# Eight activation buffer pairs of a two-layer decoder trunk, each 32 bytes longer

## The chip, the cores and the metric

The kernel runs on one core of a Trainium2 chip. The metric is the time of one execution on the device in microseconds (us), as the median of several runs. The engines are TensorE (PE, with its weight loads listed apart as PEld), VectorE (DVE), ScalarE (ACT), GpSimd (POOL) and SyncE (SP), which issues the DMAs here.

## What is computed

Two layers of a decoder trunk on 256 positions of 1024 channels, in float32. Each layer is a SwiGLU feed-forward network (FFN), a mixer, and a second FFN. The mixer of layer 0 pools over windows of 2, 4, 8 and 16 positions. The mixer of layer 1 is attention over one block of 256 positions, on keys and values that are made from the stream between the layers. The part that matters here, four times over, is

```python
def swiglu(h, w_in, w_out):
    gu = h @ w_in
    g, u = jnp.split(gu, 2, axis=-1)
    return (jax.nn.silu(g) * u) @ w_out
# D_MODEL 1024, D_FF 2816, SEQ 256; in each layer:
h = modulate(rms_norm(x, norm_g[layer, 0]), sh, sc)
x = x + MACARON_WEIGHT * (1.0 + g)[:, None, :] * swiglu(h, ffn_w_in[layer, 0], ffn_w_out[layer, 0])
```

## The kernel before

**Tiling.** Channels lie on the 128 partitions and the 256 positions along the free dimension. The 2816 inner channels of an FFN are 22 tiles of 128, numbered j. For each j the first half of an FFN (`gstep`, L464) makes one PSUM tile `gu` of 2 × 256 columns out of 8 tiles of the input `h`. `evac` (L414) makes `silu(g) * u` of it. The second half (`ystep`, L481) multiplies that by 8 weight slices of 128 × 128 (numbered m) into the four PSUM tiles `y`, which hold all 1024 output channels and are summed over the 22 j.

**Three matmuls for one.** Each float32 operand is cut into a part `hi` of type float32r and a rest `lo`. `mm3` (L255) then makes a product out of three matmuls of 256 columns: L256 streams the activation's hi over the weights' hi, L259 the activation's lo over the weights' hi, and L260 the activation's hi over the weights' lo. Each of the three loads its 128 × 128 weights (the stationary operand) and streams its activations (the moving operand) past them. The profile names them so that `y<-acth,hi` streams `acth` over the weights `hi`.

**Activation buffers.** `new_act` (L410) takes a pair `acth`, `actl` of 128 × 256 float32r from the pool `ax`, which has eight buffers of each, used in turn. ACT writes `acth` (L129, or L438 for the first three j of FFNs 1 to 3) and DVE writes `actl` (L130, L441). The pooling mixer takes its tiles `z` from the same buffers (`scaled`, L805), and `v_job` (L942) keeps the attention's values in them. There they are the stationary operand: of the matmuls `py<-at,z` (L816) and of `att<-ph,acth` (`weighted`, L989).

**Weights.** The `Stream` objects load raw weights by DMA into `raw` and cut them (L168 on ACT, L169 on DVE) into `hi` and `lo`, with two buffers of each for the first half of an FFN (8192 bytes) and two for the second (4096 bytes).

**Order.** The order on PE and SP is that of the code, and FFN starts and mixers follow the tables `PROGRAM`, `MIXER` and `ATTENTION`. In between a `g` step of 48 matmuls and a `y` step of 24 alternate; jobs such as `evac` run a step later.

**Addresses.** Within a partition the built program puts the buffers at these bytes. The eight `acth` stand 1024 bytes apart from 16576 on, and the eight `actl` from 24768 on. All sixteen leave 192 when divided by 256. All `hi` and `lo` buffers leave 160, and the weight slices in them begin at multiples of 512 bytes. The two `h` tiles `hhi` and `hlo` leave 192, with 1024 bytes from one of the 8 parts to the next, and so do the hkv tiles. The tiles `room0`, `room1` and `room2`, which nothing writes or reads, shift the buffers behind them by 64, 64 and 128 bytes.

Of the kernel before, what the change touches and what calls it, by code (L numbers as in the profile page):

```python
# [7 lines left out]
F32 = mybir.dt.float32  # L8
F32R = mybir.dt.float32r
# [4 lines left out]
P = 128  # L14
D = 1024
KT = D // P
T = 256
# [69 lines left out]
def trunk(ctx: ExitStack, tc: tile.TileContext, xin, cin, small, ada, kvada, win0a, win1a, win0b,  # L87
# [3 lines left out]
    ax = ctx.enter_context(tc.tile_pool(name="ax", bufs=8))  # L91
# [13 lines left out]
    def nm(s):  # L105
        uid[0] += 1
        return f"{s}_{uid[0]}"
# [17 lines left out]
    def psum(tag, name):  # L125
        return pp.tile([P, 512], F32, tag=tag, name=nm(name), bufs={"y": 4, "g": 3, "m": 1}[tag])
# [182 lines left out]
    def a_of(s, m):  # L309
        return acol[:, s * KT + m:s * KT + m + 1]  # L310
# [8 lines left out]
    def square2(src):  # L319

        sq = new_2t("sq")
        nc.scalar.activation(sq, src, AF.Square)
        return sq
# [9 lines left out]
    def sums(o, tiles):  # L333
        for i, sq in enumerate(tiles):
            for t in range(TT):
                nc.tensor.matmul(o[:, t:t + 1], sq[:, t * P:(t + 1) * P], ones[:, 0:1],
                                 start=(i == 0 and t == 0), stop=(i == len(tiles) - 1),
                                 skip_group_check=True)

    def rinv(acc, n, mul, add, tag="r", bufs=2):  # L340
        ms = tp.tile([P, 4], F32, tag="ms", name=nm("ms"))[:, :n]
        r = tp.tile([P, 4], F32, tag=tag, name=nm("r"), bufs=bufs)[:, :n]
        nc.vector.tensor_scalar(ms, acc, mul, add, op0=ALU.mult, op1=ALU.add)
        nc.gpsimd.tensor_tensor(r, ms, nhalf[:, :n], op=ALU.pow)  # L344
        return r
# [41 lines left out]
    def new_xa(s, n=KT):  # L387
        xh = cp.tile([P, KT, T + 2], F32R, tag="kxhi", name=nm("xah"))
        xl = cp.tile([P, KT, T + 2], F32R, tag="kxlo", name=nm("xal"))
        xa_shift((xh, xl), s, 0, n)  # L390
        return xh, xl
# [6 lines left out]
    def xa_parts(xa, m, s):  # L398
        hi = xa[0][:, m, 0:T]
        return (lambda: nc.scalar.activation(hi, xT[:, m, :], AF.Copy, scale=a_of(s, m)),  # L400
                lambda: nc.vector.scalar_tensor_tensor(
                    out=xa[1][:, m, 0:T], in0=xT[:, m, :], scalar=a_of(s, m), in1=hi.bitcast(F32),
                    op0=ALU.mult, op1=ALU.subtract))
# [4 lines left out]


    def new_act():  # L410
        return (ax.tile([P, T], F32R, tag="acth", name=nm("acth"), bufs=8),
                ax.tile([P, T], F32R, tag="actl", name=nm("actl"), bufs=8))

    def evac(act, j, ps):  # L414
        sl = tp.tile([P, T], F32, tag="sl", name=nm("sl"), bufs=3)
        act[j] = new_act()
        nc.scalar.activation(sl, ps[:, 0:T], AF.Silu)  # L417
        nc.vector.tensor_mul(sl, ps[:, T:2 * T], sl)  # L418
        hilo(sl, *act[j])
        yield  # L420
# [95 lines left out]
    def add_x(m, yv, s):  # L516
        nc.vector.scalar_tensor_tensor(out=xT[:, m, :], in0=yv, scalar=gcol[:, s * KT + m:s * KT + m + 1],
                                       in1=xT[:, m, :], op0=ALU.mult, op1=ALU.add)
# [17 lines left out]
    def fold_steps(sq):  # L536

        def fold(other):
            nc.vector.tensor_add(sq[0][:, 0, :], sq[0][:, 0, :], other())

        def pair(k, e):
            e.tensor_tensor(sq[0], sq[0], sq[k], op=ALU.add)

        return {"P1": lambda: pair(1, nc.gpsimd), "P2": lambda: pair(2, nc.gpsimd),
                "D2": lambda: pair(2, nc.vector), "D3": lambda: pair(3, nc.vector),
                "F0": lambda: fold(lambda: sq[0][:, 1, :])}

    def yview(y, m):
        return y[m // 2][:, (m % 2) * T:(m % 2 + 1) * T]

    def run(program, steps):

        split = {}
        for name in program.split():
            if name[0] == "w":
                k, piece = name[1:3], int(name[4])
                if k not in split:
                    split[k] = sa.cuts() if k[0] == "a" else [] if sb.ready else sb.cuts()
                if piece < len(split[k]):
                    split[k][piece]["hl".index(name[3])]()  # L560
            elif name in steps:
                steps[name]()
# [89 lines left out]
    with tc.tile_pool(name="xp", bufs=XBUFS) as xpool:  # L652
# [110 lines left out]
        act = {}  # L763
# [19 lines left out]
        def mixer():  # L783
            last()
            xs = cp.tile([P, KT, T], F32, tag="kxhi", name="xs")
            ss = psum("m", "ss")[:, T:T + TT]
            pw = sa.raw.pop(0)[0]
            sq, got, zps, zs, yp = {}, {}, {}, {}, {}
            steps = {}

            def group_map(g, ts=range(TT)):
                if 0 in ts:
                    zps[g] = psum("g" if g < 3 else "y", "z")
                for t in ts:
                    for i in range(2):
                        kt = 2 * g + i
                        nc.tensor.matmul(zps[g][:, t * T:(t + 1) * T], xs[:, kt, t * P:(t + 1) * P],  # L797
                                         pw[:, kt * T:(kt + 1) * T], start=(t == 0 and i == 0),
                                         stop=(i == 1), skip_group_check=True)
                if g == NG - 1:  # L800
                    sa.load()

            def scaled(g, t):

                zs[g, t] = ax.tile([P, T], F32, tag="act" + "hl"[t], name=nm("z"), bufs=8)  # L805
                nc.scalar.activation(zs[g, t], zps[g][:, t * T:(t + 1) * T], AF.Copy,
                                     scale=got["r"][:, t:t + 1])

            def pooled(g):

                yp[g] = psum("y", "py")
                for i in range(2):
                    o, c = yp[g][:, i * T:(i + 1) * T], slice(i * P, (i + 1) * P)
                    for t, to, a in ((0, slice(0, P + BAND), at[:, g, 0:P + BAND]),
                                     (1, slice(P, T), at[:, g, P + BAND:AW])):
                        nc.tensor.matmul(o[:, to], zs[g, t][:, c], a, start=(i == t == 0),  # L816
                                         stop=(t == 1), skip_group_check=True)

            def square(k):
                sq[k] = square2(xT[:, 2 * k:2 * k + 2, :])  # L820

            def begin():
                sq.clear()
                got["xa"] = new_xa(2)
                for m in range(KT):
                    steps[f"H{m}"], steps[f"L{m}"] = xa_parts(got["xa"], m, 2)

            def fold(a, b):
                nc.vector.tensor_add(a, a, b)

            steps.update(fold_steps(sq))
            steps.update({"E": lambda: fold(sq[3][:, 0, :], sq[3][:, 1, :]),
                          "F1": lambda: fold(sq[0][:, 0, :], sq[3][:, 0, :]),
                          "G2": lambda: group_map(2, [0]), "k2": lambda: group_map(2, [1])})
            for m in range(KT):
                steps[f"A{m}"] = lambda m=m: add_x(m, yview(y, m), 0)
                steps[f"X{m}"] = lambda m=m: nc.scalar.activation(xs[:, m, :], xT[:, m, :], AF.Copy,
                                                                  scale=a_of(1, m))
                steps[f"B{m}"] = lambda m=m: add_x(m, yp[m // 2][:, m % 2 * T:(m % 2 + 1) * T], 1)
            for g in range(NG):  # L840
                steps[f"Q{g}"] = lambda g=g: square(g)
                steps[f"g{g}"] = lambda g=g: group_map(g)
                steps[f"y{g}"] = lambda g=g: pooled(g)
                for t in range(TT):
                    steps[f"z{g}{t}"] = lambda g=g, t=t: scaled(g, t)
            steps.update({"S": lambda: sums(ss, [sq[0][:, 0, :]]),
                          "R": lambda: got.update(r=rinv(ss, TT, 1.0 / D, EPS)), "N": begin})
            run(MIXER, steps)
            return {k: steps[k] for k in ("L6", "L7")}, got["xa"], lambda: [sq[0][:, 0, :]]
# [90 lines left out]
    def v_job(c, pv):  # L940
        for t in range(TT):
            vt[c, t] = new_act()  # L942
            hilo(pv[:, t * T:(t + 1) * T], *vt[c, t])
        yield
# [207 lines left out]
```

## Time and profile before

| | us |
|---|---|
| median of 3 runs | 897.16 |
| the three runs | 894.82, 897.16, 897.55 |
| the profiled execution | 894.96 |
| its span, first to last instruction | 892.8 |
| PE busy / DVE busy / ACT busy in it | 879.4 / 717.1 / 453.0 |

All that is said of the trace comes from the profiled execution. Its time is 2.2 us over its span, and 2.2 us under the median of the runs. In the page, a matmul's listed duration (around 0.28 us) is longer than the distance to the next one's start, since matmuls are pipelined. So what one matmul costs is read from the starts: two starts in the timeline, and the number of matmuls between them.

### The profile page before, as it was taken

How to read it: one execution, taken by the hardware profiler on the slowest of the kernel's cores; microseconds unless marked ns; L12 is line 12 of the kernel's file. 1: busy time of each engine (PE TensorE's matmuls, PEld its weight loads, DVE VectorE, ACT ScalarE, POOL GpSimd, SP SyncE). 2: the span in 40 equal slices, each digit the busy share in tenths (PEclk: the TensorE clock that was granted, in tenths of full speed). 3: DMA queues.
4: the chain of work that ended last, by engine and by line, in shares of the span. 5: the costliest groups of instructions: out<-in, count | busy, mean ns of one | idle time of the engine just before them, and what ended most of it. 6: DMA issues, size and time to landing. Idle time of an engine off the chain costs nothing.

```text
span 892.8 us, 17826 instructions
## 1 busy us (share of the span) xinstructions
PE 879.4 (99%) x7398; PEld 873.0 (98%) x7398; DVE 717.1 (80%) x1212; ACT 453.0 (51%) x721; POOL 49.4 (6%) x52
## 2 busy tenths in 40 slices
PE   6999999999999999999999999999999999999998
PEld 4999999999999999999999999999999999999998
DVE  5988988878998878869998888789888894665553
ACT  3456344328744444457554443457676674443431
POOL 0000000002000000000000000034431100000000
PEclk9999999999999999999999999999999999999999
DMA  9987998784799998554989899664534377656521
GB/s 349 421 346 282 419 381 353 286 325 148 271 419 416 373 335 323 175 206 167 370 314 388 334 374 372 234 238 184 178 107 127 111 269 274 228 174 204 175 72 48
DMA packets 41699, 240.32 MB, mean 269 GB/s; under 512 B 4625, under 2 KB 5009, under 8 KB 20370
## 3 DMA queue, kind: packets, MB, share of 16 engines
q1 hardware_dynamic: 41618, 239.18, 71.0%
q8 instruction: 58, 0.95, 0.4%
q14 instruction: 23, 0.19, 0.1%
HBM read 238.11 MB, written 1.05 MB: 268 GB/s over the span
## 4 chain that ended last, share of the span: by engine, by line
PE 93%; DVE 4%; DMA 1%; ACT 1%; POOL 1%; issue 0%; DVEq 0%; SPq 0%; POOLq 0%
PE gu L256 18%; PE gu L260 18%; PE gu L259 18%; PE y L259 10%; PE y L256 10%; PE y L260 10%; DVE lo L169 1%; PE gu L721 1%; PE pj L256 1%; PE pj L259 1%; PE pj L260 1%; DMA rawA<-in_ada_dram 1%; PE z L797 1%; DVE rawA L264 1%; POOL r L344 1%
## 5 line engine op out<-in xcount | busy, mean ns | idle before, releaser
L168 ACT CAST hi<-raw 128x1024 fp32r<-128x1024 f32 (+1 forms) x322 | 302.5, 974 | 322.5 <-PE gu L259 219.6
L169 DVE TENSOR_TENSOR lo<-raw,hi 128x1024 fp32r<-128x1024 f32 (+1 forms) x322 | 355.6, 1132 | 126.5 <-ACT hi L168 123.2
L256 PE MATMUL gu<-hhi,hi 128*128 128x256 f32 x1248 | 348.4, 279 | 0.0
L260 PE MATMUL gu<-hhi,lo 128*128 128x256 f32 x1248 | 348.3, 279 | 0.0
L259 PE MATMUL gu<-hlo,hi 128*128 128x256 f32 x1248 | 348.2, 279 | 0.0
L260 PEld LDWEIGHTS gu<-hhi,lo 128*128 128x128 f32 x1248 | 234.6, 188 | 0.1
L256 PEld LDWEIGHTS gu<-hhi,hi 128*128 128x128 f32 x1248 | 234.6, 188 | 0.0
L259 PEld LDWEIGHTS gu<-hlo,hi 128*128 128x128 f32 x1248 | 234.6, 188 | 0.0
L260 PE MATMUL y<-acth,lo 128*128 128x256 f32 x704 | 196.4, 279 | 0.0
L259 PE MATMUL y<-actl,hi 128*128 128x256 f32 x704 | 196.4, 279 | 0.0
L256 PE MATMUL y<-acth,hi 128*128 128x256 f32 x704 | 196.4, 279 | 0.0
L256 PEld LDWEIGHTS y<-acth,hi 128*128 128x128 f32 x704 | 132.3, 188 | 0.0
L259 PEld LDWEIGHTS y<-actl,hi 128*128 128x128 f32 x704 | 132.3, 188 | 0.0
L260 PEld LDWEIGHTS y<-acth,lo 128*128 128x128 f32 x704 | 132.3, 188 | 0.0
L264 DVE CUSTOM_DVE_ANT_0 rawX<-rawX,cb 128x1024 f32<-128x1024 f32 x80 | 94.6, 1219 | 0.4 <-DMA rawX<-in_ada_dram 0.4
L417 ACT ACTIVATE sl<-gu 128x256 f32<-128x256 f32 x79 | 29.2, 375 | 38.0 <-PE gu L260 36.0
L418 DVE TENSOR_TENSOR sl<-gu,sl 128x256 f32<-128x256 f32 x79 | 32.8, 419 | 12.7 <-ACT sl L417 12.7
L256 PE MATMUL gu<-xah,hi 128*128 128x258 f32 x144 | 41.3, 287 | 0.0
L259 PE MATMUL gu<-xal,hi 128*128 128x256 f32 x144 | 40.7, 283 | 0.0
L260 PE MATMUL gu<-xah,lo 128*128 128x258 f32 x144 | 40.7, 283 | 0.0
L129 ACT CAST acth<-sl 128x256 fp32r<-128x256 f32 x79 | 31.9, 406 | 13.1 <-DVE sl L418 11.4
L130 DVE TENSOR_TENSOR actl<-sl,acth 128x256 fp32r<-128x256 f32 x79 | 33.0, 419 | 1.6 <-ACT acth L129 1.6
(146 smaller groups left out, 999.9 us busy)
## 6 DMA issues: line engine op xcount, KB each, us to landing
raw<-in_win1b_dram SPq DMA_DIRECT2D x57, 1024.0 KB, 6.2
raw<-in_wout_dram SPq DMA_DIRECT2D x88, 512.0 KB, 6.3
rawX<-in_ada_dram SPq DMA_DIRECT2D x34, 1024.0 KB, 8.7
raw<-in_win1a_dram SPq DMA_DIRECT2D x14, 1024.0 KB, 10.1
rawA<-in_ada_dram SPq DMA_DIRECT2D x12, 1024.0 KB, 7.0
kxhi<-in_ada_dram SPq DMA_DIRECT2D x11, 1024.0 KB, 8.3
kxlo<-in_ada_dram SPq DMA_DIRECT2D x10, 1024.0 KB, 8.9
raw<-in_win0b_dram SPq DMA_DIRECT2D x12, 768.0 KB, 4.3
```

What stands on the lines that cost most here:

```text
L129: i = nc.scalar.copy(hi, src)
L130: nc.vector.tensor_tensor(lo, src, hi.bitcast(F32), op=ALU.subtract)
L168: return [(lambda a=a, b=b: after_anchor(nc.scalar.copy(hi[:, a:b], raw[:, a:b])), lambda a=a, b=b: nc.vector.tensor_tensor(lo[:, a:b], ra ...
L169: lambda a=a, b=b: nc.vector.tensor_tensor(lo[:, a:b], raw[:, a:b], hi[:, a:b].bitcast(F32), op=ALU.subtract)) for a, b in cut]
L256: i = nc.tensor.matmul(o, wh, xh, start=start, stop=False, skip_group_check=True)
L259: nc.tensor.matmul(o[:, 0:T], wh, xl, start=False, stop=False, skip_group_check=True)
L260: nc.tensor.matmul(o, wl, xh, start=False, stop=stop, skip_group_check=True)
L264: i = nc.vector.tensor_tensor_reduce(out=v, in0=v, in1=cb, scale=1.0, scalar=0.0, op0=ALU.mult, op1=ALU.add, accum_out=mb[:, col:col + 1])
L344: nc.gpsimd.tensor_tensor(r, ms, nhalf[:, :n], op=ALU.pow)
L417: nc.scalar.activation(sl, ps[:, 0:T], AF.Silu)
L418: nc.vector.tensor_mul(sl, ps[:, T:2 * T], sl)
L721: nc.tensor.matmul(g0[j][:, half * T:(half + 1) * T], w0[:, (2 * j + half) * P:(2 * j + half + 1) * P], h0, start=(half == 0), stop=False, ...
```

## The change

`new_act` allocates 264 float32r (1056 bytes) per partition for each buffer in place of 256 (1024 bytes) and hands out the first 256 of them. The tiles `z` of the pooling mixer, which use the same tags and buffers, are made likewise. Nothing reads or writes the last 32 bytes. In the built program the order of instructions on each engine and the waits are the same as before; only addresses differ.

```diff
     def new_act():
-        return (ax.tile([P, T], F32R, tag="acth", name=nm("acth"), bufs=8),
-                ax.tile([P, T], F32R, tag="actl", name=nm("actl"), bufs=8))
+        return tuple(ax.tile([P, T + 8], F32R, tag=k, name=nm(k), bufs=8)[:, 0:T] for k in ("acth", "actl"))
...
             def scaled(g, t):
 
-                zs[g, t] = ax.tile([P, T], F32, tag="act" + "hl"[t], name=nm("z"), bufs=8)
+                zs[g, t] = ax.tile([P, T + 8], F32, tag="act" + "hl"[t], name=nm("z"), bufs=8)[:, 0:T]
```

The eight `acth` now stand at 16576, 17632, 18688, 19744, 20800, 21856, 22912 and 23968, the eight `actl` at 25024 and so on in the same steps. Modulo 256 both rows read 192, 224, 0, 32, 64, 96, 128, 160. Everything behind them, weights and `h` among it, moves by 512 bytes, so that its remainder modulo 256 stays.

In this document the distance of a matmul is the start of its streamed operand minus the start of its stationary operand, modulo 256 bytes. The 2112 matmuls of `y` over activation buffers stand like this (counted in the built programs):

| distance | 0 | 32 | 64 | 96 | 128 | 160 | 192 | 224 |
|---|---|---|---|---|---|---|---|---|
| matmuls before | 0 | 2112 | 0 | 0 | 0 | 0 | 0 | 0 |
| matmuls after | 264 | 264 | 240 | 240 | 264 | 264 | 288 | 288 |

## Rows read from the trace of the kernel before

**Rows 1.** The page, part 1: busy us, share of the span, instructions.

```profile
PE 879.4 (99%) x7398; PEld 873.0 (98%) x7398; DVE 717.1 (80%) x1212; ACT 453.0 (51%) x721; POOL 49.4 (6%) x52
```

**Rows 2.** The page, part 2: granted TensorE clock in 40 slices of the span.

```profile
PEclk9999999999999999999999999999999999999999
```

**Rows 3.** The page, part 4: share of the span in the chain that ended last.

```profile
PE 93%; DVE 4%; DMA 1%; ACT 1%; POOL 1%; issue 0%; DVEq 0%; SPq 0%; POOLq 0%
```

**Rows 4.** Waits of PE, all of them: us in total, times, longest.

```profile
PE cb L633 <- DMA crow<-in_c_dram: 2.4, 1, 2.4
PE rbk L350 <- POOL r L344: 2.1, 1, 2.1
PE rb L350 <- POOL r L344: 2.0, 1, 2.0
PE gu L721 <- ACT h L718: 1.5, 1, 1.5
PE ss L336 <- DVE sq L693: 0.9, 1, 0.9
PE y L259 <- DVE hlo L130: 0.4, 1, 0.4
```

**Rows 5.** Groups of instructions by line and shape, PE.

```profile
L260 PE MATMUL y<-acth,lo 128*128 128x256 f32 x704 | 196.4, 279 | 0.0
L259 PE MATMUL y<-actl,hi 128*128 128x256 f32 x704 | 196.4, 279 | 0.0
L256 PE MATMUL y<-acth,hi 128*128 128x256 f32 x704 | 196.4, 279 | 0.0
```

**Rows 6.** Timeline of PE, two y steps: start us, duration us, instruction.

```profile
310.32 0.28 PE L256 MATMUL y<-acth,hi 128*128 128x256 f32 x1
...
315.80 0.28 PE L260 MATMUL y<-acth,lo 128*128 128x256 f32 x1
315.92 0.28 PE L256 MATMUL gu<-hhi,hi 128*128 128x256 f32 x1
```

**Rows 7.** Timeline of PE, end of the g step behind it.

```profile
321.40 0.28 PE L260 MATMUL gu<-hhi,lo 128*128 128x256 f32 x1
321.52 0.28 PE L256 MATMUL y<-acth,hi 128*128 128x256 f32 x1
```

**Rows 8.** Timeline of PE, one values step (stationary hkv, streamed weights).

```profile
640.26 0.28 PE L259 MATMUL v<-lo,hkvh 128*128 128x256 f32 x1
...
645.70 0.28 PE L260 MATMUL v<-hi,hkvl 128*128 128x256 f32 x1
645.82 0.28 PE L256 MATMUL s<-kh,qh 128*128 128x256 f32 x1
```

**Rows 9.** Timeline of PE, two attention steps over the values.

```profile
674.29 0.28 PE L256 MATMUL att<-ph,acth 128*128 128x256 f32 x1
...
675.00 0.38 PE L983 MATMUL pT<-ident,p 128*128 128x128 f32 x2
...
679.90 0.29 PE L256 MATMUL att<-ph,acth 128*128 128x256 f32 x1
...
680.62 0.28 PE L256 MATMUL y<-hhi,hi 128*128 128x256 f32 x1
```

**Rows 10.** Timeline of PE, an FFN start on xah and xal.

```profile
222.12 0.28 PE L259 MATMUL gu<-xal,hi 128*128 128x256 f32 x1
222.24 0.28 PE L260 MATMUL gu<-xah,lo 128*128 128x258 f32 x1
...
231.74 0.28 PE L256 MATMUL gu<-hhi,hi 128*128 128x256 f32 x1
```

**Rows 11.** Timeline of PE, attention scores of two heads, then of one.

```profile
654.21 0.28 PE L259 MATMUL s<-kl,qh 128*128 128x256 f32 x1
...
655.54 0.28 PE L256 MATMUL pj<-hhi,hi 128*128 128x256 f32 x1
...
668.76 0.28 PE L256 MATMUL s<-kh,qh 128*128 128x256 f32 x1
...
669.47 0.27 PE L983 MATMUL pT<-ident,p 128*128 128x128 f32 x1
```

**Rows 12.** Timeline of PE, three transposes of 128 columns.

```profile
661.86 0.49 PE L983 MATMUL pT<-ident,p 128*128 128x128 f32 x3
662.19 0.50 PE L909 MATMUL hs<-ones,sq 128*128 128x1 f32 x4
```

**Rows 13.** Writers of acth and actl: ns min/median/max, first and last start.

```profile
L129 ACT CAST acth<-sl x79: 391/407/423, 60.8 to 878.5; 128x256 fp32r<-128x256 f32 x79
L130 DVE TENSOR_TENSOR actl<-sl,acth x79: 414/418/428, 61.4 to 879.0; 128x256 fp32r<-128x256 f32 x79
```

## Prediction

> **What bounds the kernel now.** I read the busy times first: TensorE is busy for 99% of the span, and no other engine is near it [rows 1]. Then the granted clock, which is full in all 40 slices, that is 2.4 GHz throughout, so no part of the time is lost to a lower clock [rows 2]. Then the chain of work that ended last, which is TensorE for 93% [rows 3], and TensorE's waits, which are six and add up to 9.3 us [rows 4]. None of the six is a wait for an activation buffer. So the time is the number of matmuls times the distance in time from one start to the next. A change that touches that spacing shows in the total one for one, and one that touches anything else has cover.
>
> The listed 279 ns of a matmul [rows 5] do not tell the spacing. Two y steps start at 310.32 us and the next g step at 315.92 us, with 48 matmuls between: 5.60 us / 48 = 116.7 ns [rows 6]. That g step ends at 321.52 us, 48 matmuls later: again 116.7 ns [rows 6, 7]. Both have the distance 32 (192 − 160), in all three matmuls of each product.
>
> Now the places where the trace shows other distances. In the values step the streamed weights leave 160 and the stationary hkv tiles 192, so the distance is 224 in every matmul. From 640.26 to 645.82 us there are 47 matmuls: 5.56 / 47 = 118.3 ns [rows 8]. In the attention over the values, streamed ph and pl and stationary acth and actl all leave 192, so the distance is 0. Six matmuls take 0.71 us in one place and 0.72 us in the other, 118.3 and 120.0 ns, 119.2 in the mean [rows 9]. At the start of an FFN the streamed tiles xah and xal have rows of 1032 bytes, so the distance grows by 8 bytes from one channel tile to the next: 128 to 184 for xah, 192 to 248 for xal. From 222.12 to 231.74 us there are 80 of them, 120.2 ns each [rows 10]. Two in three stream 258 columns and not 256; at 116.7/256 ns a column that is 0.6 ns in the mean, which leaves 119.6. In the scores, distances run from 96 to 152 (kh) and 160 to 216 (kl): 11 matmuls in 1.33 us, 120.9 ns, and 6 in 0.71 us, 118.3 ns [rows 11]. **Every stretch at another distance than 32 is slower than those at 32**, by 1.6 (224), 2.5 (0), 3.0 (128 to 248 mixed) and 1.6 to 4.2 ns (96 to 216 mixed).
>
> **The change part by part.** No instruction is added, removed or moved, and no wait. What changes is the distance of the 2112 matmuls of y over activation buffers [rows 5]: 264 stay at 32, and 1848 go to seven other distances, 240 to 288 at each.
>
> *The y matmuls.* At 224, 288 matmuls at the 1.63 ns of the values step [rows 6, 8]: 0.47 us. At 0, 264 at the 2.5 ns of the attention [rows 9]: 0.66 us. For 96, 128, 160 and 192 the trace has only stretches in which the three matmuls of a product stand at two distances; for 64 it has none. These five hold 240 + 240 + 264 + 264 + 288 = 1296 matmuls. Their price is bounded by nothing below (as at 32) and by 4.2 ns above, the dearest of the score stretches [rows 11]: 0 to 5.4 us. I take 2.0 ns, 2.6 us, about midway between 1.63 and 2.5. The values step and the attention are the nearest rows, since in them, as in y, all three matmuls of a product share one distance and starts lie on multiples of 32 bytes; the FFN start has starts that are off by 8 bytes besides. The sum is 0.47 + 0.66 + 2.59 = **3.7 us more**, with ends of 1.1 and 6.6 us.
>
> *The writers of the buffers.* ACT and DVE write acth and actl at the new addresses, 96 of each, 79 of them in one form. The trace has one remainder only. The nearest bound is the spread of the same operation at one address: 391 to 423 and 414 to 428 ns [rows 13]. Should every cast become as slow as the slowest, that is 16 ns × 96 = 1.5 us of ACT in 893 us, and less on DVE. It lies under TensorE, which nowhere waits for these buffers [rows 4]; without that cover it would be the 1.5 us. I cost it at nothing.
>
> *The tiles as stationary operand.* The 48 attention matmuls over the values leave the distance 0 for eight others; between 2.5 ns less and 1.7 ns more for each (4.2 against 2.5), that is −0.12 to +0.08 us. The pooling mixer's 32 matmuls over z are fewer still, and the same prices give less than 0.15 us. Nothing for either.
>
> *All else* moves by 512 bytes and keeps its distance. Within each y step of before, the weight slices already stand at eight multiples of 512 from one activation buffer, and the step keeps one spacing (5.60 us for two of them [rows 6]), so this is nothing too.
>
> **A rule against this reading.** The rows show a spacing that goes with the distance: 118.3 ns at 224 against 116.7 ns at 32 [rows 6, 8]. The Trainium skill, page "TensorE: Matmul & The Clock Gate", section "Step-by-step: what each phase is for", says that TensorE has two independent read ports into SBUF, one for the streamed operand and one for the weight loads, so that loading the next weights takes no bandwidth from the running matmul. By that rule, where the two operands stand relative to each other would make no difference, and the sum would be nothing. The trace speaks against it in so far as two kinds of matmul of the same size differ; what it does not exclude is that something else than the distance divides them, and that is the first rival.
>
> **The rivals.**
> *Not the distance (no change).* The slower stretches have other things in common than their distance. In the values step and the attention, what was computed is the stationary operand and not the streamed one; the FFN start streams 258 columns and odd starts; the attention and the scores are short, with other kinds of matmul around them. If one of these is the cause of each, y stays at 116.7 ns and the time at 897.2. For it: no row shows one kind of matmul at two aligned distances. Against it: four different excuses are needed for four stretches, while one distance unites g and y, whose streamed tiles, weight buffers and outputs all differ and which both have 116.7 ns. It decides if the y steps after show one spacing whatever their buffer.
> *Few bad distances (within the noise).* Only 0 and 224, for which rows stand, cost something, and the other five are as good as 32. That is 1.1 us more, 898.3. Against it are the slower mixed stretches, which cover 96 to 216.
> *The dear price.* Each of the seven costs what the FFN start shows, 3.0 ns: 1848 × 3.0 = 5.5 us, 902.7. At the 4.2 ns of the scores it is 7.8 us, 904.9. For it: 96 to 248 are measured there and nowhere else. Against it: the two distances in one product and the starts off by 8 bytes.
> *Faster.* 116.7 ns may not be the least that loading 128 × 128 weights and streaming 256 columns can take: transposes, whose loads are as large, follow each other after 0.33/3 = 110 ns [rows 12]. If the five distances without a clean row ran at 110 ns, 1296 × 6.7 = 8.7 us would go, less the 1.1 us of the other two: 889.6. This needs that clean groups at 96 to 192 do the opposite of the mixed ones; if 64 alone did it, 240 × 6.7 = 1.6 us would go against 3.1 us paid elsewhere, and it would still be slower.
>
> **How the numbers follow.** The profiled execution took 894.96 us, which gives 898.7 for it; the median of the runs shown is 2.2 us higher, at 897.16, and the forecast is made for that: 897.16 + 3.7 = **900.9 us**. About 0.3%, here 2.7 us, is what a measurement of this kernel can tell from no change. Chances: the forecast 0.53; the dear price 0.15; few bad distances 0.14; not the distance 0.13; faster 0.05. The range goes from 897.2 (no change) to 904.9 (all seven at the dearest row), which leaves out the faster case and half of the no-change case. Slower by over 0.3%: 0.53 + 0.15 = 0.68. Within it: 0.14 + 0.13 = 0.27. Faster: 0.05.
>
> **What would show it.** In the profile after, the spacing inside a y step of 24 matmuls should differ from step to step, in a cycle of eight as the buffers come round: 116.7 ns (2.80 us a step) at 32, about 118.3 (2.84 us) at 224, about 119.2 (2.86 us) at 0, and about 118.7 (2.85 us) for the other five. The g steps should stay at 116.7 ns (5.60 us), PE's waits at some 9 us, and the clock full. If all y steps still take 2.80 us, the distance is not the cause; if some take less, 116.7 is no floor; if g steps grow, the shift by 512 bytes or the writers matter, which I have put at nothing.

## The result and the profile after

The changed kernel takes 902.64 us (three runs: 901.36, 902.64 and 902.76) against 897.16 us before. The ratio is 1.0062, with an interval from 1.0046 to 1.0077. The forecast was 900.9 us in a range from 897.2 to 904.9, and slower by over 0.3%.

The page of the changed kernel shows the same bound as before [rows 1], with TensorE busy for longer and the rest as it was:

```profile
span 900.7 us, 17826 instructions
PE 887.0 (98%) x7398; PEld 880.7 (98%) x7398; DVE 717.2 (80%) x1212; ACT 451.7 (50%) x721; POOL 49.6 (6%) x52
```

TensorE's waits are still six, 9.4 us together, and none is for an activation buffer, as in [rows 4]. (Columns: total us, times, longest.)

```profile
PE rbk L350 <- POOL r L344: 2.2, 1, 2.2
PE cb L632 <- DMA crow<-in_c_dram: 2.2, 1, 2.2
PE rb L350 <- POOL r L344: 2.0, 1, 2.0
PE gu L720 <- ACT h L717: 1.5, 1, 1.5
PE ss L336 <- DVE sq L692: 1.2, 1, 1.2
PE y L259 <- DVE hlo L130: 0.4, 1, 0.4
```

So the loss is in the spacing of matmuls. Below is one full cycle of the eight buffers in the second FFN: the first matmul of each y step and of each g step, in the timeline of TensorE (start us, duration us). The y steps stand at the distances 224, 192, 160, 128, 96, 64, 32, 0 in this order, then 224 again; each g step between them is at 32.

```profile
244.03 0.28 PE L256 MATMUL y<-acth,hi 128*128 128x256 f32 x1
...
246.86 0.28 PE L256 MATMUL gu<-hhi,hi 128*128 128x256 f32 x1
...
252.47 0.28 PE L256 MATMUL y<-acth,hi 128*128 128x256 f32 x1
...
255.20 0.28 PE L256 MATMUL gu<-hhi,hi 128*128 128x256 f32 x1
...
260.80 0.28 PE L256 MATMUL y<-acth,hi 128*128 128x256 f32 x1
...
263.63 0.28 PE L256 MATMUL gu<-hhi,hi 128*128 128x256 f32 x1
...
269.23 0.28 PE L256 MATMUL y<-acth,hi 128*128 128x256 f32 x1
...
272.07 0.28 PE L256 MATMUL gu<-hhi,hi 128*128 128x256 f32 x1
...
277.72 0.28 PE L256 MATMUL y<-acth,hi 128*128 128x256 f32 x1
...
280.59 0.29 PE L256 MATMUL gu<-hhi,hi 128*128 128x256 f32 x1
...
286.26 0.28 PE L256 MATMUL y<-acth,hi 128*128 128x256 f32 x1
...
289.08 0.28 PE L256 MATMUL gu<-hhi,hi 128*128 128x256 f32 x1
...
294.84 0.28 PE L256 MATMUL y<-acth,hi 128*128 128x256 f32 x1
...
297.72 0.28 PE L256 MATMUL gu<-hhi,hi 128*128 128x256 f32 x1
...
303.48 0.28 PE L256 MATMUL y<-acth,hi 128*128 128x256 f32 x1
...
306.36 0.28 PE L256 MATMUL gu<-hhi,hi 128*128 128x256 f32 x1
...
312.01 0.28 PE L256 MATMUL y<-acth,hi 128*128 128x256 f32 x1
```

The difference of two neighbours is the length of a step. At 116.7 ns, a y step of 24 matmuls takes 2.80 us and a g step of 48 takes 5.60 us [rows 6, 7]. Here:

| distance of the y step | 224 | 192 | 160 | 128 | 96 | 64 | 32 | 0 |
|---|---|---|---|---|---|---|---|---|
| y step, us | 2.83 | 2.73 | 2.83 | 2.84 | 2.87 | 2.82 | 2.88 | 2.88 |
| the g step behind it, us | 5.61 | 5.60 | 5.60 | 5.65 | 5.67 | 5.76 | 5.76 | 5.65 |
| mean of all y matmuls at it, ns | 118.1 | 114.3 | 117.6 | 118.4 | 119.6 | 117.9 | 119.4 | 119.8 |

Two things were not foreseen. The g steps, whose operands kept their distance of 32, run at up to 120.0 ns (5.76/48). And the one distance that was kept, 32, is among the slowest for y, while 192 is quicker than any y or g step of the kernel before.

**The sum.** Start to start, over the whole trace, the 2112 y matmuls take 249.3 us against 246.3 before, and the 3744 matmuls of g over h take 440.8 against 437.2. That is 3.0 + 3.6 = 6.6 us. The profiled executions differ by more, 902.76 − 894.96 = 7.8 us, since that of the changed kernel has a stretch at half the granted clock (1.2 GHz), some 1.5 us after TensorE had stood idle for 2.25 us, from 628 us on, waiting for POOL's `r`:

```profile
626.00:631.00 5.00, 2.75 (x25) 1.00 0.12 21
631.00:636.00 5.00, 5.00 (x32) 0.66 0.51 195
636.00:660.00 24.00, 24.00 (x209) 1.00 0.45 154
```

(Columns: stretch, its length in us, PE's busy us with the number of matmuls, granted clock, DMA share, GB/s.) 15 matmuls there follow each other after 213 ns and not 117, and one on either side of them is longer in part, which costs 1.5 us together. It is not the change's doing: in 39 of the 42 runs of the kernel before that were taken later, the mean granted clock is 0.997 to 0.999 too; its profiled execution, at 1.0, had no such stretch. The difference of the medians is 5.5 us. The two executions of the changed kernel with a mean clock of 1.0 lie 901.36 − 894.96 = 6.4 and 902.64 − 894.96 = 7.7 us over the profiled one of the kernel before. The 6.6 us lies among these.

### The profile page after: what moved, and what is told of

It is laid out like the page before. It is cut to its first block, busy times and chain, and to the rows that moved or that the text cites. A ratio compares the mean times of both kernels' runs of the same rounds, so it can differ in the third digit from the quotient of the medians.

```text
span 900.7 us, 17826 instructions
## 1 busy us (share of the span) xinstructions
PE 887.0 (98%) x7398; PEld 880.7 (98%) x7398; DVE 717.2 (80%) x1212; ACT 451.7 (50%) x721; POOL 49.6 (6%) x52
## 4 chain that ended last, share of the span: by engine, by line
PE 93%; DVE 4%; DMA 1%; ACT 1%; POOL 1%; issue 0%; DVEq 0%; SPq 0%; POOLq 0%
PE gu L256 18%; PE gu L260 18%; PE gu L259 18%; PE y L259 10%; PE y L256 10%; PE y L260 10%; DVE lo L169 1%; PE gu L720 1%; PE pj L256 1%; PE pj L260 1%; PE pj L259 1%; DMA rawA<-in_ada_dram 1%; PE z L796 1%; DVE rawA L264 1%; POOL r L344 1%
```

## The experiments

All but one move buffers and do nothing else: the number of elements in the unused tiles `room0` (ahead of the activation buffers), `room1` (ahead of the weights) and `room2` (ahead of h) is changed in the kernel before, and the activation buffers keep their 1024 bytes. The weights always leave 160 modulo 256. "Theory A" is that a distance has a steady spacing of its own; "theory B" that it has several, of which the matmuls before pick one. (The expectation for all y at 64 uses "theory A" otherwise: there it means that a y step at 64 hands a slow spacing on to the g step behind it.)

### All y at 192

```diff
-    ax.tile([P, 16], F32, tag="room0", name="room0", bufs=1)
+    ax.tile([P, 56], F32, tag="room0", name="room0", bufs=1)
-    cp.tile([P, 16], F32, tag="room1", name="room1")
+    cp.tile([P, 40], F32, tag="room1", name="room1")
```

> The kernel before with its activation buffers moved as a block, still 1024 bytes apart, so that every y matmul over them stands at distance 192; the tiles h stay at 32. Theory A (each distance has its own steady spacing, and 192 is a fast one): y steps at 113.9 ns as in the profile after, 2.8 ns x 2112 = 5.9 us less, g steps at 116.7 ns, about 891.3 us against 897.2. Rival (the quick steps at 192 come only from the change from one distance to the next): y back at 116.7 ns, 897 us.

Measured: 891.85 us, ratio 0.9945 (0.9924 to 0.9966). Its timeline, y, g and the next y:

```profile
250.24 0.28 PE L256 MATMUL y<-acth,hi 128*128 128x256 f32 x1
...
252.98 0.28 PE L256 MATMUL gu<-hhi,hi 128*128 128x256 f32 x1
...
258.58 0.28 PE L256 MATMUL y<-acth,hi 128*128 128x256 f32 x1
```

The y step takes 2.74 us, 114.2 ns a matmul, and the g step 5.60. The quick steps at 192 do not come from the change of distance between neighbouring buffers; 116.7 ns is no floor. And since the buffers have their old length here, the length is not what makes these steps quick.

### All y at 64

```diff
-    ax.tile([P, 16], F32, tag="room0", name="room0", bufs=1)
+    ax.tile([P, 24], F32, tag="room0", name="room0", bufs=1)
-    cp.tile([P, 16], F32, tag="room1", name="room1")
+    cp.tile([P, 8], F32, tag="room1", name="room1")
```

> The same block move, to distance 64 for every y matmul; h stays at 32. Theory A (a step hands its state on: after a step at 64, a step at 32 runs at 120 and not at 116.7 ns): y at 117.8 ns, 1.2 x 2112 = 2.5 us more, and the some 63 g steps behind a y step at 119.9 ns, 63 x 48 x 3.3 = 9.9 us more, about 909.5 us. Rival (each matmul pays by its own distance alone, and what g paid in the changed kernel has another cause): g at 116.7 ns, 899.7 us.

Measured: 890.81 us, 0.9934 (0.9909 to 0.9959). Neither expectation held: 909.5 and 899.7 us were both far off, and so was the sign.

```profile
250.10 0.28 PE L256 MATMUL y<-acth,hi 128*128 128x256 f32 x1
...
252.83 0.28 PE L256 MATMUL gu<-hhi,hi 128*128 128x256 f32 x1
...
258.44 0.28 PE L256 MATMUL y<-acth,hi 128*128 128x256 f32 x1
```

The y step takes 2.73 us, 113.6 ns, where the same distance took 117.9 ns in the changed kernel; the g step takes 5.61 us. One distance, two spacings, though only the activation buffers have moved here, by 32 bytes. So something besides the distance decides, and theory A falls here. That it is the matmuls before is seen further down, where 64 runs both ways in one kernel.

### Everything at 192

```diff
 # as for y at 192, and
-    hp.tile([P, 32], F32, tag="room2", name="room2")
+    hp.tile([P, 8], F32, tag="room2", name="room2")
```

> Activation buffers and both h tiles moved, so that y, g and the q, k and output projections all stand at distance 192, the values step at 64. Theory A (113.6 ns is the steady spacing at 192): 6432 matmuls x 3.1 = 19.9 us less and 0.1 us less in the values steps, about 877 us, if no other engine becomes the bound. Rival (192 is quick only beside other distances): 897 us. A second rival: VectorE, busy for 80% of the span, or the loads of weights become the bound, and waits of TensorE give some of it back: 877 to 890 us.

Measured: 894.43 us, 0.9956 (0.9927 to 0.9985), but from 888.8 to 901.14 us in ten runs, in groups near 889 (four runs), 895 (five) and 901 (one). The profile, of a run at 895.05 us, points to the reason. First a g and a y stretch of the first FFN, then the same in the second FFN:

```profile
114.08 0.28 PE L256 MATMUL gu<-hhi,hi 128*128 128x256 f32 x1
...
119.52 0.28 PE L256 MATMUL y<-acth,hi 128*128 128x256 f32 x1
...
124.96 0.28 PE L256 MATMUL gu<-hhi,hi 128*128 128x256 f32 x1
```

```profile
250.54 0.28 PE L256 MATMUL gu<-hhi,hi 128*128 128x256 f32 x1
...
256.20 0.28 PE L256 MATMUL y<-acth,hi 128*128 128x256 f32 x1
...
259.02 0.28 PE L256 MATMUL gu<-hhi,hi 128*128 128x256 f32 x1
```

A g step takes 5.44 us (113.3 ns) and two y steps 5.44 us in the first FFN; in the second, 5.66 us (117.9 ns) and 2.82 us for one. Same instructions, same distance: one spacing holds through one FFN and the other through the next three. Each of the last three FFNs has 19 × 48 + 22 × 24 = 1440 such matmuls, so one FFN in the slow spacing costs 1440 × 4.5 ns = 6.5 us. The means of the groups of runs lie 5.5 and 6.4 us apart, which fits one FFN more or less in the slow spacing; only this run was profiled, so it is not shown for the others. VectorE and the loads did not become the bound: TensorE's waits are the same six, 10.0 us together.

### All y at 0, and all y at 128

```diff
-    ax.tile([P, 16], F32, tag="room0", name="room0", bufs=1)
+    ax.tile([P, 8], F32, tag="room0", name="room0", bufs=1)
-    cp.tile([P, 16], F32, tag="room1", name="room1")
+    cp.tile([P, 24], F32, tag="room1", name="room1")
 # 40 and 56 for the distance 128
```

> The activation buffers as a block at distance 0, h at 32. Theory B (the spacing at a distance is one of several, and the matmuls before pick it; a y step at 0 leaves the g step behind it at 117.9 ns, as seven g steps in the profile of the changed kernel have it): y at 119.8 ns, 3.1 x 2112 = 6.5 us more, and some 63 g steps x 48 x 1.2 ns = 3.6 us more, about 907.3 us. Rival (the g steps there had taken over a slow spacing from steps at 32 and 64 further back, and 0 leaves nothing): g at 116.7 ns, 903.7 us.

Measured: 905.26 us, 1.0093 (1.0068 to 1.0117).

```profile
253.64 0.28 PE L256 MATMUL y<-acth,hi 128*128 128x256 f32 x1
...
256.51 0.28 PE L256 MATMUL gu<-hhi,hi 128*128 128x256 f32 x1
...
262.17 0.28 PE L256 MATMUL y<-acth,hi 128*128 128x256 f32 x1
```

2.87 us for y (119.6 ns) and 5.66 us for the g step behind it (117.9 ns): 63 of its 71 g steps run like this, in all four FFNs, though neither the h tiles nor the weights have moved by a byte in this kernel. A y step at 0 slows the g step behind it by itself. The measured time is 2 us below the sum of theory B and 1.6 above the rival's; by the trace, y takes 6.6 us and g 3.7 us more than before, which are theory B's two terms.

> The block at distance 128, h at 32. Theory B: y at 118.4 ns, 1.75 x 2112 = 3.7 us more; the g steps behind it at 116.8 ns if they only pass on what came before (as in the first FFN of the changed kernel), about 900.9 us, or at 117.8 ns if a step at 128 itself leaves them slow (as in its later FFNs), 3.3 us more, 904.2 us. Rival (a distance has one spacing): 118.4 and 116.7 ns, 900.9 us, the same in all four FFNs.

Measured: 901.47 us, 1.0053 (1.0036 to 1.0071). y runs at 118.2 to 118.8 ns, but for the first step (120.1), and g at 116.6 to 116.9 in all FFNs. So 128 alone does not slow the g steps. What made them 117.8 ns (5.65 us) behind it in the changed kernel must lie further back than the y step before them; it was not isolated.

### 96 and 64 in turn, and 96 alone

```diff
+    pairs = [0]
+
     def new_act():
-        return (ax.tile([P, T], F32R, tag="acth", name=nm("acth"), bufs=8),
-                ax.tile([P, T], F32R, tag="actl", name=nm("actl"), bufs=8))
+        k = pairs[0] % 2
+        pairs[0] += 1
+        if pairs[0] == 2:
+            ax.tile([P, 56], F32, tag="room3", name="room3", bufs=1)
+        return tuple(ax.tile([P, T], F32R, tag=f"{n}{k}", name=nm(n), bufs=4) for n in ("acth", "actl"))
 # room0 32 and room1 8 elements; z takes the same buffers by g % 2
```

> Two blocks of four pairs, used in turn: every second y step stands at 96, the others at 64, h at 32. In the changed kernel 64 came behind 96 and ran at 117.8 ns; alone it ran at 113.5. Theory B (the state that 96 leaves decides): y at 64 at 117.8 ns and at 96 at 119.6, 4.3 us more, and the g steps behind 64 at 119.9 and behind 96 at up to 118.0 ns, 5 to 7 us more: 906 to 908 us. Rival (the g steps between wipe out what a y step leaves, and the slow 64 has another cause): y at 113.5 and 119.6 ns, g at 116.7 to 116.9, about 897 us.

Measured: 905.24 us, 1.0099 (1.0072 to 1.0126), 0.8 us under the range of theory B and 8 us over the rival. In the second FFN, from a y step at 64: g, y at 96, g, y at 64.

```profile
253.34 0.28 PE L256 MATMUL y<-acth,hi 128*128 128x256 f32 x1
...
256.17 0.28 PE L256 MATMUL gu<-hhi,hi 128*128 128x256 f32 x1
...
261.92 0.28 PE L256 MATMUL y<-acth,hi 128*128 128x256 f32 x1
...
264.79 0.28 PE L256 MATMUL gu<-hhi,hi 128*128 128x256 f32 x1
...
270.39 0.28 PE L256 MATMUL y<-acth,hi 128*128 128x256 f32 x1
```

64 takes 2.83 us (117.9 ns) and leaves the g step at 5.75 us (119.8 ns); 96 takes 2.87 us and leaves 5.60. That is the link of the changed kernel, 96 then 64 then a g step at 120, cut out and shown alone. In the first FFN, where two y steps follow each other without a g step, 64 shows both its spacings within 11 us:

```profile
94.14 0.28 PE L256 MATMUL y<-acth,hi 128*128 128x256 f32 x1
...
96.97 0.28 PE L256 MATMUL gu<-hhi,hi 128*128 128x256 f32 x1
...
102.57 0.28 PE L256 MATMUL y<-acth,hi 128*128 128x256 f32 x1
...
105.44 0.28 PE L256 MATMUL y<-acth,hi 128*128 128x256 f32 x1
...
108.17 0.28 PE L256 MATMUL gu<-hhi,hi 128*128 128x256 f32 x1
```

At 94.14 us it stands behind a g step and takes 2.83 us; at 105.44 us it stands right behind 96 and takes 2.73. Nor does every slow 64 slow the g step behind it: the one at 96.97 us takes 5.60 us, where the second FFN has 5.75 behind a y step of the same distance and the same spacing. So neither the distance nor the spacing of the step before is the whole state.

> The block at 96, h at 32. Either theory: y at 119.6 to 120.0 ns, 6.3 us more. What it leaves to the g steps tells which link of the chain is the bad one: 116.7 ns (as in the first FFN of the changed kernel), 903.5 us, or 118.0 ns (as in its later ones), 4 us more, 907.5 us.

Measured: 903.64 us, 1.0081 (1.0052 to 1.011). y runs at 119.7 to 120.0 ns. The g steps run at 117.8 ns in the first FFN and at 116.6 in the others. Both expected values occur, in one kernel. 96 alone is thus slow for y and leaves g one or the other.

### h at 64, h at 192, and both moved

The rest put the larger share of the matmuls, g and the projections over h (4320 with those of the output), at the two distances that have a quick spacing.

```diff
-    hp.tile([P, 32], F32, tag="room2", name="room2")
+    hp.tile([P, 40], F32, tag="room2", name="room2")
 # 40: h at 64; 8: h at 192. With y at 192: room0 56, room1 40; with y at 64: 24 and 8
```

> The h and hkv tiles at 64, the activation buffers at 32 as before. Theory B with the quick spacing of 113.4 ns at 64, which y had behind steps at 32: 3.3 x (3744 g + 384 projections + 192 output projections) = 14.3 us less, about 882.9 us, y still at 116.7 ns. Rival (64 falls into its slow spacing of 117.8 ns, as in the changed kernel): 1.1 x 4320 = 4.8 us more, 902 us, or some FFNs each way.

> h and hkv at 64 and the activation buffers at 192, so that each step changes between two distances which both have a quick spacing. Theory B, if both stay quick: a further 3.0 x 2112 = 6.3 us below the kernel with h alone at 64, about 876.6 us. If the state at an FFN's start is held through that FFN, as in the kernel with 192 everywhere: 117.8 ns in some FFNs and 113.3 in others, some 6 us for each slow one, 877 to 901 us, differing from run to run. Rival (only a change to or from 32 makes a step quick): 897 us or more.

> h and hkv at 192, the activation buffers at 64, both with a quick spacing of 113.3 to 113.5 ns and a slow one of 117.8. Quick loop throughout: 876.5 us; slow throughout: about 904 us; an FFN held in one or the other, by some 6 us each, gives values in between that differ from run to run. Rival (one distance, one spacing): 876.5 us in every run.

> h and hkv at 192, the activation buffers at 32. Theory B: a loop of two distances settles into one of few states. Quick one: g and projections at 113.4 ns, 3.2 x 4320 = 13.8 us less, 883.4 us. Slow one: 117.8 ns, 4.8 us more, 902 us. FFNs may differ, and so may runs. Rival (192 holds its quick spacing always when the other distance is 32, as it did for y): 883.4 us in every run.

| h / y at | us, lowest to highest | ratio, interval | g, ns, by FFN | y, ns, by FFN |
|---|---|---|---|---|
| 64 / 32 | 894.20 (893.28 to 898.49) | 0.9981 (0.9965 to 0.9997) | 113.4, 113.4, 117.8, 117.8 | 117, 117, 116.6, 116.6 |
| 64 / 192 | 900.84 (899.28 to 903.09) | 1.0044 (1.0028 to 1.006) | 117.8 in all | 117.7, 113.6, 117.6, 117.7 |
| 192 / 64 | 894.62 (891.64 to 902.21) | 0.9985 (0.9964 to 1.0006) | 113.5, 113.5, 117.7, 117.7 | 117.8 in all |
| 192 / 32 | 886.84 (886.21 to 887.72) | 0.9897 (0.9875 to 0.9919) | 113.7 in all | 116.8 in all |

(Spacings are those of most steps of an FFN, in the profiled run.) A pair of distances settles into a loop and mostly stays in it; which one may differ from FFN to FFN, and with it the time from run to run. The quick spacing throughout, with its sums of 882.9, 876.6 and 876.5 us, came out in none of the first three. With h at 192 and y at 32, every FFN of the profiled run found its quick loop, though in three of them two or three g steps at the start run at 117.8 ns. The four runs lie within 1.5 us, less than the 19 × 48 × 4.1 ns = 3.7 us that the g steps of one FFN in the slow spacing would cost. The timeline shows y, g, y:

```profile
250.02 0.28 PE L256 MATMUL y<-acth,hi 128*128 128x256 f32 x1
...
252.82 0.28 PE L256 MATMUL gu<-hhi,hi 128*128 128x256 f32 x1
...
258.28 0.28 PE L256 MATMUL y<-acth,hi 128*128 128x256 f32 x1
```

2.80 us for y and 5.46 us for g (113.8 ns). At 886.84 us this kernel, the one before with `room2` 96 bytes shorter, beats both: by 1.0% the one before and by 1.75% (886.84 / 902.64) the changed one, on the medians. It came 3.4 us short of its expected 883.4: over the whole trace its g matmuls take 114.6 ns each (429.1 us), and not 113.4.

**Distance, or the place of the streamed tile alone?** The weights leave 160 in every kernel here, so y and g cannot tell these two apart. The values steps can: there the weights stream, from 160 in all kernels, and the hkv tiles that stand still were moved. At distance 224 they take 118.3 ns [rows 8]. In the kernel with h and hkv at 64 (hkv leaves 224), the distance of the values steps is 192:

```profile
637.66 0.28 PE L259 MATMUL v<-lo,hkvh 128*128 128x256 f32 x1
...
642.99 0.28 PE L256 MATMUL s<-kh,qh 128*128 128x256 f32 x1
```

47 matmuls take 5.33 us, 113.4 ns; the first and the last of the four values steps run at 117.8. These are the two spacings of y and g at 192. In the three kernels with h and hkv moved to 192 (hkv leaves 96, and the distance of the values steps is 64) they all run at 117.8 ns. And y at 0, which streams from 160 as well, over weights at 160, takes 119.8. So the place relative to the stationary tile counts.

## Why the prediction was right, and where it was not

**What bounds the kernel** held. TensorE is busy throughout, its waits did not change (9.4 us against 9.3), and apart from the stretch at half the clock the time moved with the spacing of its matmuls.

**The y matmuls** were to cost 3.7 us; they cost 3.0. The two terms with clean rows were near: 118.1 ns at 224 (118.3 forecast) and 119.8 at 0 (119.2 forecast). The 2.0 ns taken for the five others came out as 1.2 (64), 3.0 (96), 1.7 (128), 0.9 (160) and −2.4 (192). Taking the price at 32 as the bound from below was wrong: 192 is quicker than 32, as the rival "faster" had it for distances in general. Also wrong was to cost the 264 matmuls that stay at 32 at nothing: they run at 119.4 ns, 2.7 × 264 = 0.7 us.

**"All else keeps its distance"** is the step that failed. It costed the 3744 g matmuls at nothing, because nothing of theirs moves modulo 256. They cost 3.6 us, more than y. The step's own reason was sound for an address and unsound for a state: the experiments with y at 0, and with 96 and 64 in turn, show g steps at 117.9 and 119.8 ns with operands at their old distance, by what the steps before them left. The text had said that if g steps grew, the shift by 512 bytes or the writers would matter. Neither does: with y at 0 nothing behind the activation buffers is shifted at all, and the waits show no writer.

The trace of the kernel before already had a sign of it. One projection over hkv, at the distance 32 as all of them, is not at the 116.7 ns of [rows 6, 7]:

```profile
604.48 0.28 PE L259 MATMUL pj<-hkvl,hi 128*128 128x256 f32 x1
...
609.90 0.28 PE L260 MATMUL pj<-hkvh,lo 128*128 128x256 f32 x1
```

46 matmuls in 5.42 us are 117.8 ns; the other seven projections, at the same distance, run at 116.6 to 116.8. So a step at 32 could be slow with nothing of it moved. The rows at 32 that the prediction chose had one spacing; the trace had two.

**The total**, 900.9 forecast and 902.64 measured, is thus right in sign and inside the range, 1.7 us low. Two errors partly cancel: y was put 0.7 us too high and g 3.6 us too low. That the total stayed within the range is luck in part, since the range's upper end, 904.9, was worked out from the y matmuls alone and held no term for g.

**The rivals.** "Not the distance" is out: a block move of the buffers alone gives 890.8 to 905.3 us, and the values steps change with the place of the stationary tile. "Few bad distances" is out, since 96, 128 and 32 itself pay as well. "The dear price", 902.7 us, has the right total and the wrong place. "Faster" is the one that had more in it than its chance: not in this change, but a placement of one distance can be quicker than before.

**The rule of the two read ports.** With instructions and order unchanged, y averages between 113.5 ns (all at 64) and 119.8 (all at 0). The rule that the prediction cites (the Trainium skill, page "TensorE: Matmul & The Clock Gate", section "Step-by-step: what each phase is for"), read as the prediction reads it, would have the placement make no difference, and this reading does not hold here. Whether the two ports share anything is not shown.

**What stays open.** What carries the state from one step to the next is not seen. The mean spacing of a g step does not tell it: at 94.14 us above, 64 ran slowly behind a g step of 116.7 ns, and in the kernel with y at 64 it ran quickly behind 116.9. Which loop an FFN falls into at its start was not tried apart. The 32 bytes of length with all distances kept were not tried either; the kernels with the old length that show the same spacings at 192, 128, 96 and 0 speak against a part for it. That distances count modulo 256 was assumed; it fits that y and g of the kernel before, whose distances are 288 and 32 modulo 512, both run at 116.7 ns.

## What to carry to other kernels

When TensorE bounds a kernel with a weight load for every matmul, where the streamed operand starts relative to the weights is a setting like any other, worth up to 1% here for no instruction at all. It cannot be costed matmul by matmul: a step at a bad distance can slow well-placed steps behind it, so measure the steps beside a change, and over several runs, since a placement can have more than one steady spacing. A rotation over many distances is no safe way around a bad one (902.64 us here; single distances for y gave 890.8 to 905.3): it makes the matmuls visit them all, and the bad ones can slow the steps behind.

## What the runs showed of the hardware

With 128 × 128 weights and 256 float32r columns at a granted clock of 1.0, steady steps run at 113.3, 116.7 or 120.0 ns a matmul, or at means between. At 2.4 GHz these three are 272, 280 and 288 cycles, 8 apart. The distance of 32 was seen with all of 116.7, 117.8 and 120.0 ns, 64 with 113.4 and 117.8, 192 with 113.3 and 117.8; 0 and 96 were never seen below 119 in a whole y step of 24. A spacing held through a whole FFN, 1440 matmuls, when nothing changed the distance. And some 1.5 us after an idle time of 2.25 us, TensorE's granted clock fell to half for about 3 us, 1.5 us of time, in the changed kernel's profiled execution. It did not in that of the kernel before, nor in that of the kernel with everything at 192, where TensorE waited 2.1 and 2.7 us at the same place.
